# An encoder block on one core: row weights on K, three Q/K chains interleaved, gate weights ahead of branches, the last gate group by token halves

## The chip, the core and the metric

The kernel runs on one core of one Trainium2 chip. The engines are TensorE (PE in the profile; its weight loads are PEld), VectorE (DVE), ScalarE (ACT), GpSimd (POOL) and SyncE (SP), which here issues every DMA. The metric is the device time of one execution in microseconds (us), lower is better.

## The reference

One layer of an encoder on 1024 tokens (a grid of 16 rows by 64 columns), width 1024, all in float32:

```
u = rmsnorm(x) * g1
q, k, v, cb, cc, ch, ga, gb = split(u @ w_in)     # 512 each, ga and gb 1024 each
q = rmsnorm(q per head) * gq ; k = rmsnorm(k per head) * gk       # 8 heads of 64
p = softmax(q k^T / 8 + bias) in a window of 8 rows x 16 columns, clamped to the grid
y_a = (p v) @ w_a                                  # attention branch
y_b = (cb * conv3(cc * ch)) @ w_b                  # convolution branch
x = x + (sigmoid(ga) * y_a + sigmoid(gb) * y_b) @ w_o
x = x + relu(rmsnorm(x) * g2 @ w1)^2 @ w2          # feed-forward width 4096
```

## The kernel before, in words

**Split products.** Every large product is taken in float16 with float32 sums. Each operand is scaled by a power of two and split into a high half (ScalarE writes the rounded copy) and a low half (VectorE subtracts the high half from the scaled value, `scalar_tensor_tensor`). Three matmuls per tile pair (`PASSES`) add high-high, high-low and low-high. A *unit* is the matmuls of one output tile in one PSUM bank; `unit()` issues them, counts them in `units`, and then runs pending work of the other engines. Text and profile call such groups units: 24 matmuls in the projections, 12 in the gates and branches.

**Order of the work.** The whole order is written out: Python generators yield between instructions and are advanced by hand. `fg` holds work that follows a unit (`step()` advances every generator of it by one), `bg` holds the preparation of weights (`tick()` advances the first one, and, where `side` is set, the next ones while the first yields `WAIT`). `unit(mms, post, steps, ticks)` settles the `post` of the unit before, then takes `steps` steps and `ticks` ticks in turn. `apart(mark, n)` yields `WAIT` until `units` has reached `mark + n`; `flush()` runs `bg` empty with such waits set aside (`forced`). Each engine takes its instructions in the order of issue.

**Weights.** `plan()` gives the order of the weight pieces. `load_upto` loads them in that order into a ring of five raw buffers (`raw`, L205, on SP's queue); a piece is loaded when `done` counts enough split pieces (L205 can then wait for its buffer). `Chunk.prep` (L236 to L285) makes the scale of a chunk: for Q, K, the convolution and gate 0 by sums of squares over rows (L236 squares on ScalarE, L239 the sum), the sum over partitions by a matmul with ones (L176), `pow2_half` (L399 to L406) and the row scale (L248); then it splits the pieces (L285 high, L273 low). Between the sum of rows and the matmul with ones stands `yield from apart(units[0])`, three units. For the branches, w_o and V the scale comes from largest values (L296 to L306).

**Stages.** (1) Norm of x, transposes (L432 by DMA for blocks 3 to 7), V; from x also four *token forms* (sums and differences of quarters, `sforms`, L469 the scaled copies, L476 on GpSimd, L478 high, L480 low half, L482 stored to `GS` in DRAM), which the gates use. (2) Q: 8 units, K: 8 units. Each has a chain `qk_vec` behind it: copy (L570), squares (L571), sums per head (L574), reciprocal root (L385 to L394), a scale `sgq` for Q (L578), product (L581), the gains gq times gk for Q (L584), high half (L588, `q16`; for Q written twice), low half (L590); `finish_qk` then transposes the block by DMA (L601). (3) Two convolution units, then attention in 64 steps with the convolution's matmuls among them (180 to 357 us). (4) Gate stage: eight groups n of 128 columns; each has gate units, then four branch units. Group 0 is taken directly, groups 1 to 7 by seven products instead of eight (Strassen and Winograd): `prep_s` scales and adds raw weights (L973, L941), sums them, and splits them (L960 high, L954 low); `seven()` issues units 1, 6, 5, 4, 2, 7, 3, each with an activation form f and a weight form w. `turn_s` brings the stored forms back transposed (L909); form f = 2 lies where half of u was, and comes after group 0's gates. `post7` and `post3` close the group, `sigmoid` (L1026) runs over all four quarters. (5) Group 7 takes its branches first, into `y`; `last()` multiplies gate and y and `m_split` splits the result (L994, L996) into `M`. (6) Projection w_o in two column halves of eight token blocks; the first two units issue 21 of 24 matmuls each before the three that need group 7. Norm and the feed-forward part (from about 690 us) follow.

Of the kernel before, what the change touches and what calls it, by code (L numbers as in the profile page):

```python
# [10 lines left out]
F32 = mybir.dt.float32  # L11
F16 = mybir.dt.float16
# [3 lines left out]
OP = mybir.AluOpType  # L16
# [5 lines left out]
HD = 64  # L22
# [6 lines left out]
def plan():  # L29


    def block(w, groups, per=2, tiles=8, first=0):
        return [(w, first + k, per, groups) for k in range(0, tiles, per)]

    p = [(("V", j), block("w_in", [(1024 + 256 * j, 256)], 4)) for j in range(2)]
    p += [(("Q", 0), block("w_in", [(0, 512)])), (("K", 0), block("w_in", [(512, 512)]))]
    p += [(("C", j), block("w_in", [(c + 128 * j, 128) for c in (2048, 2560, 1536)])) for j in range(4)]
    branch = lambda j: [((k, j), block(w, [(256 * j, 256)], 4, 4)) for k, w in (("A", "w_a"), ("B", "w_b"))]
    for n in range(8):
        p.append((("S" if n else "G", n), block("w_in", [(3072 + 128 * n, 128), (4096 + 128 * n, 128)], 4)))  # L40
        if n in (0, 1, 3, 5):
            p += branch((n + 1) // 2)
    p += [(("O", j), block("w_o", [(512 * j, 512)])) for j in range(2)]
    for q in range(16):
        p.append((("1", q), block("w_1", [(128 * q, 128), (2048 + 128 * q, 128)], 4)))
    for s in range(4):
        p.append((("2", s), [("w_2", 4 * s + k, 2, [(c, 512)]) for c in (0, 512) for k in (0, 2)]))
        p.append((("X", s), [("w_2", 16 + 4 * s + k, 2, [(c, 512)]) for c in (0, 512) for k in (0, 2)]))
    return p
# [3 lines left out]
def encoder_block(ctx: ExitStack, tc: tile.TileContext, x, weights, cols, gqk, g2, rel, masks, out):  # L53
# [161 lines left out]
    class Chunk:  # L215
# [9 lines left out]
        def prep(self):  # L225
# [5 lines left out]
            if self.kind in "QKCG":  # L231
                self.parts = wsp.tile([128, 2, tot], F16, name="w16_ws", tag="ws")
                for p, (k, w) in enumerate(self.widths):
                    while len(self.raw) <= p:
                        yield WAIT
                    A.activation(self.parts[:, 1, :k * w].bitcast(BF16), self.raw[p][:, :k * w], AF.Square,  # L236
                                 accum_out=sc[:, at(rm, p)])
                    yield
                V.tensor_reduce(sc[:, a], sc[:, at(rm, 0, n)], axis=AX, op=OP.add)  # L239
                c = ones_col()  # L240
                V.tensor_tensor(c, sc[:, a], sc[:, gm2], op=OP.mult)
                yield from apart(units[0])
                yield from all_sum(c, b, bank(self.bank) if self.bank else anybank(), 1e-36)
                yield from pow2_half(b, 14, s, self.inv, more=self.more)
            else:
                yield from self.largest(rm, a, b)
                yield from pow2(b, 14, s, self.inv, False, more=self.more)
# [211 lines left out]
    turned, formed = [0], [0]  # L459
    SFORM = (5, 8, 10, 12)  # L460

    def sforms():

        for n, start in enumerate(SFORM):
# [3 lines left out]
            for b in (n, n + 4):  # L468
                A.activation(xt[:, b], xt[:, b], AF.Copy, scale=sc[:, at(ys, b)])  # L469
                z += [xt[:, b, :512], xt[:, b, 512:]]  # L470
            yield
            f = wqk.tile([128, 4, 512], F32, name="sform", bufs=1)
            v = wqk.tile([128, 4, 2, 512], F16, name="s16", bufs=2)
            for o, a, b, op in ((2, z[0], z[2], OP.subtract), (0, z[2], z[3], OP.subtract),
                                (1, f[:, 0], z[0], OP.subtract), (3, z[1], f[:, 1], OP.add)):
                G.tensor_tensor(f[:, o], a, b, op=op)  # L476
            yield from apart(units[0], 1 + (start < 6))
            A.activation(v[:, :, 0], f, AF.Copy)  # L478
            yield
            V.tensor_tensor(v[:, :, 1], f, v[:, :, 0], op=OP.subtract)  # L480
            yield from apart(units[0], 1)
            SP.dma_start(GS[:, n], v)  # L482
            formed[0] = n + 1

# [82 lines left out]
    def qk_vec(ps, inv, kind, res):  # L567
        qs = wqk.tile([128, 512], F32, name="qs", bufs=2)
        sq = wqk.tile([128, 512], F32, name="sq", bufs=1)
# [5 lines left out]
        yield  # L575
        yield from rstd(ss, HD, y, 0 if kind == "q" else 12)
        if kind == "q":
            V.tensor_scalar(sc[:, y], sc[:, y], sc[:, sgq], None, op0=OP.mult)  # L578
            yield
        q3 = qs.rearrange("p (h d) -> p h d", h=8)  # L580
        V.tensor_tensor(q3, q3, sc[:, y][:, :, None].to_broadcast([128, 8, HD]), op=OP.mult)  # L581
        yield
        if kind == "q":
            V.tensor_tensor(q3, q3, gq[:, 0][:, None, :].to_broadcast([128, 8, HD]), op=OP.mult)  # L584
        r = 2 if kind == "q" else 1
        t = wqk.tile([128, 8, 2, r, HD], F16, name=kind + "16")
        q4 = q3[:, :, None, :].to_broadcast([128, 8, r, HD])
# [15 lines left out]
    for n, (kind, b) in enumerate(todo):  # L603
# [6 lines left out]
        def post(ps=ps, kind=kind, n=n, ch=ch):  # L610
            fg.append(qk_vec(ps, ch.inv, kind, q16[n]))
        unit(tok_mms(ps, actU, b, ch, 8, 512, 0), post, 6, 3)
        if n == 3:
# [368 lines left out]

    def seven(P, act, c0, c1, posts, steps, ticks):

        ps = {}
        for i, f, w in ((1, 0, 0), (6, 4, 5), (5, 2, 3), (4, 3, 6), (2, 1, 1), (7, 5, 4), (3, 6, 2)):
            ps[i] = anybank()[:, c0:c1]
            post = posts.get(i)
            unit(group(ps[i], [(P[:, w, sw, k * 128:k * 128 + 128], act(f, sa, k)[:, c0:c1])
                               for k in range(4) for sw, sa in PASSES]),  # L990
                 post and (lambda post=post: post(ps)), steps, ticks)
# [13 lines left out]
    def gate_units(n, tail=None):  # L1005
# [12 lines left out]
        def post7(ps):  # L1018
            V.tensor_tensor(z[2], ps[7], z[1], op=OP.add)
            V.tensor_tensor(z[1], z[3], z[1], op=OP.subtract)  # L1020
            V.tensor_tensor(z[3], z[3], z[2], op=OP.subtract)
            V.tensor_tensor(z[2], ps[4], z[2], op=OP.add)

        def post3(ps):
            V.tensor_tensor(z[1], ps[3], z[1], op=OP.add)
            A.activation(sg, sg, AF.Sigmoid, scale=sc[:, cS[n].inv])  # L1026
            if tail:
                tail()
        seven(cS[n].P, actS, 0, 512, {
# [3 lines left out]
            2: lambda ps: V.tensor_tensor(z[0], ps[2], z[0], op=OP.add),  # L1033
            7: post7, 3: post3}, 2, 4 if n < 7 else 6)
        return sg
# [10 lines left out]
    for n in range(8):  # L1046
        built(cG if n == 0 else cS[n])
        if n < 7:
            bg.insert(len(bg) if n == 0 else 0, prep_s(n + 1))
        if n in (2, 4):  # L1050
            push(cA[n // 2 + 1], cB[n // 2 + 1])
        m = w3p.tile([128, 2, 512], F32, name="m", bufs=1)
        mf = m.rearrange("p a t -> p (a t)")
        if n < 7:
# [9 lines left out]
            branch_units(n, post)  # L1064
            if n == 0:
                push(cA[1], cB[1])
            late.append(lambda n=n, mf=mf: fg.append(m_done(n, mf)))
        else:
# [20 lines left out]

            def last():  # L1090
                for half in range(2):
                    o = slice(2 * half, 2 * half + 2)
                    V.tensor_tensor(sg7[0][:, o], sg7[0][:, o], y[:, o], op=OP.mult)
                    V.tensor_tensor(m[:, half], sg7[0][:, 2 * half], sg7[0][:, 2 * half + 1], op=OP.add)
                fg.append(m_split(7, mf, s7))
            sg7 = []
            sg7.append(gate_units(7))
            X1 = base.tile([128, 8, D], F32, name="x1", tag="Q")
            for b in range(8):
                SP.dma_start(X1[:, b], x[b * 128:(b + 1) * 128, :])  # L1100
            settle()
            last()
    drain()
# [128 lines left out]
    two = []  # L1232
    for b in range(2):
        proj(b, 0, None, two)
    unit(two[0][0][:21])
    unit(two[1][0][:21])
    for mm, fin in two:
        unit(mm[21:], fin, 6, 3)
    for b in range(2, 8):
        proj(b, 0)  # L1240
# [311 lines left out]
```

## Time and profile before

| what | us |
|---|---|
| median of 3 runs (1317.94 to 1324.43) | 1320.93 |
| the profiled execution, its time | 1319.66 |
| its span, first to last instruction | 1317.9 |
| TensorE busy | 1226.5 (93%) |
| VectorE busy | 970.5 (74%) |
| ScalarE busy | 717.3 (54%) |
| GpSimd busy | 442.1 (34%) |

Busy times by stretch of the span (us; the clock is the granted TensorE clock as a share of full speed):

| stretch | stage | TensorE | VectorE | ScalarE | clock |
|---|---|---|---|---|---|
| 68 to 118 | Q | 45.3 of 50 | 34.2 | 30.0 | 0.93 |
| 118 to 180 | K, two convolution units | 55.2 of 62 | 49.6 | 37.6 | 0.94 |
| 180 to 357 | attention | 159.0 of 177 | 133.6 | 120.0 | 0.99 |
| 357 to 388 | gate group 0 | 31.0 of 31 | 11.3 | 18.1 | 1.00 |
| 388 to 432 | group 1, start of 2 | 37.8 of 44 | 30.3 | 21.9 | 0.92 |
| 432 to 598 | groups 2 to 7 | 166.0 of 166 | 120.1 | 74.9 | 1.00 |
| 598 to 690 | w_o | 85.5 of 92 | 64.6 | 36.6 | 0.98 |
| 690 to 1318 | norm, feed-forward | 595.3 of 628 | 485.6 | 333.1 | 0.97 |

A busy TensorE is not a TensorE at full speed: after an idle time matmuls show a lower clock and take longer. In a line of the profile, `L273` is a line of the kernel, `w_ws<-raw` says that it writes tile w_ws from raw, and a bracket gives the idle time of the engine before it and what ended it.

### The profile page before, as it was taken

The numbers are of one execution on the slowest core, as the hardware profiler recorded it, in microseconds if no ns is written. First come the engines' busy times: TensorE is split into PE (matmuls) and PEld (weight loads), VectorE is DVE, ScalarE is ACT, GpSimd is POOL, SyncE is SP. The second block draws the span as 40 slices with busy tenths as digits, with TensorE's granted clock in tenths as the row PEclk, the third lists the DMA queues.
The fourth block names the chain that finished last, engine by engine and source line by source line (L and its number), as shares of the span: only waits on it lengthen the run. The fifth ranks groups of instructions, "written<-read, shape, count | busy, mean of one in ns | idle before, by whom it ended". The sixth has DMA issues, their size and how long they took to land.

```text
span 1317.9 us, 16922 instructions
## 1 busy us (share of the span) xinstructions
PE 1226.5 (93%) x6294; PEld 581.5 (44%) x6294; DVE 970.5 (74%) x1747; ACT 717.3 (54%) x1057; POOL 442.1 (34%) x269
## 2 busy tenths in 40 slices
PE   5987998988998999998997899999999799999998
PEld 3533444444443444443445644444444344444443
DVE  6567867878646877665779777777846578889797
ACT  5765666667455555522445556655564664546530
POOL 2430001211121221100202587777837307080562
PEclk8989999999999999999997999999999899999999
DMA  6645545555653212105346554445461862626212
GB/s 242 143 148 116 117 105 125 119 96 128 125 111 96 78 39 64 44 21 207 96 93 135 148 175 132 163 147 176 176 239 67 270 253 69 251 96 240 68 60 96
DMA packets 170946, 173.86 MB, mean 132 GB/s; under 512 B 131440, under 2 KB 131952, under 8 KB 166768
## 3 DMA queue, kind: packets, MB, share of 16 engines
q1 hardware_dynamic: 170864, 172.79, 44.2%
q8 instruction: 49, 0.80, 0.2%
q14 instruction: 33, 0.27, 0.1%
HBM read 103.03 MB, written 37.75 MB: 107 GB/s over the span
## 4 chain that ended last, share of the span: by engine, by line
PE 48%; DVE 21%; ACT 12%; issue 9%; DMA 6%; POOL 2%; SPq 1%; ACTq 0%; DVEq 0%; POOLq 0%
PE ps_s L184 16%; PE ps_d L184 15%; PE ps_o L184 11%; PE ps_d L847 4%; DMA PT<-P 3%; DVE w L954 3%; ACT as L1257 2%; ACT w L960 2%; DVE as L1284 2%; DVE w_ws L273 1%; POOL sform L476 1%; DMA raw<-in_weights 1%; DVE v L1157 1%; DVE as L1289 1%; PE ps_s L771 1%
## 5 line engine op out<-in xcount | busy, mean ns | idle before, releaser
L184 PEld LDWEIGHTS <-w 128*128 128x128 f16 x1512 | 149.8, 100 | 163.9 <-issue 18.3
L184 PEld LDWEIGHTS <-ops 128*128 128x128 f16 x1356 | 133.2, 99 | 174.3 <-issue 19.0
L1124 POOL TENSOR_TENSOR as<-as 128x512 f32<-128x512 f32 x64 | 109.1, 1705 | 85.1 <-ACT as L1259 81.4
L847 PE MATMUL ps_d<-uT,w_ws 128*128 128x512 f16 x528 | 127.2, 382 | 0.9 <-ACT w_ws L285 0.8
L184 PE MATMUL ps_s<-ops 128*128 128x512 f16 (+1 forms) x528 | 119.7, 377 | 3.7 <-DVE x L1483 2.0
L184 PE MATMUL ps_d<-ops 128*128 128x512 f16 x492 | 113.4, 380 | 0.0
L941 POOL TENSOR_TENSOR tsum<-raw 128x512 f32<-128x512 f32 x32 | 57.9, 1827 | 146.4 <-DVE mL L996 68.1
L184 PEld LDWEIGHTS <-uT 128*128 128x128 f16 x648 | 65.9, 102 | 82.0 <-issue 22.9
L184 PEld LDWEIGHTS <-w_s 128*128 128x128 f16 x588 | 57.3, 99 | 78.6 <-issue 4.6
L184 PE MATMUL ps_d<-u2T,w 128*128 128x512 f16 (+1 forms) x396 | 85.7, 367 | 4.8 <-DVE as L1288 4.8
L1257 ACT ACTIVATE as<-as 128x2048 f32<-128x2048 f32 x16 | 30.6, 1910 | 108.7 <-DVE as L1292 108.7
L1373 ACT ACTIVATE ops<-hf,sc 128x2048 f16<-128x2048 f32 x26 | 51.9, 1997 | 67.2 <-PE ps_d L184 25.1
L184 PE MATMUL ps_o<-ops 128*128 128x512 f16 x336 | 79.9, 388 | 8.9 <-DVE ops L1382 4.7
L954 DVE SCALAR_TENSOR_TENSOR w<-raw,sc,w 128x512 f16<-128x512 f32 (+1 forms) x32 | 43.3, 1359 | 56.3 <-ACT w L960 56.2
L1375 DVE SCALAR_TENSOR_TENSOR ops<-hf,sc,ops 128x2048 f16<-128x2048 f32 x26 | 70.2, 2699 | 12.8 <-ACT ops L1373 12.8
L847 PEld LDWEIGHTS <-w_ws 128*128 128x128 f16 x528 | 51.1, 98 | 56.4 <-issue 3.3
L1388 POOL TENSOR_TENSOR raw<-raw 128x1024 f32<-128x1024 f32 x8 | 24.8, 3095 | 142.8 <-DVE ops L1382 142.8
L941 POOL TENSOR_TENSOR gsum<-raw 128x512 f32<-128x512 f32 x14 | 18.6, 1329 | 138.9 <-ACT raw L973 138.9
L184 PE MATMUL ps_d<-w_ws,uT 128*128 128x512 f16 x192 | 49.3, 410 | 11.5 <-DVE w_ws L273 8.1
L954 DVE SCALAR_TENSOR_TENSOR w<-tsum,sc,w 128x1024 f16<-128x1024 f32 x32 | 59.5, 1896 | 0.0
L184 PE MATMUL ps_s<-u2T,w 128*128 128x512 f16 (+1 forms) x252 | 50.0, 350 | 2.8 <-DVE form L1150 2.8
L941 POOL TENSOR_TENSOR tsum<-tsum,raw 128x512 f32<-128x512 f32 x32 | 46.1, 1439 | 18.1 <-ACT tsum L936 16.8
(290 smaller groups left out, 2591.9 us busy)
## 6 DMA issues: line engine op xcount, KB each, us to landing
raw<-in_weights SPq DMA_DIRECT2D x92, 512.0 KB, 3.8
hs<-as SPq DMA_DIRECT2D x16, 1792.0 KB, 6.8
hf<-hs SPq DMA_DIRECT2D x26, 1024.0 KB, 9.5
w2x<-in_weights SPq DMA_DIRECT2D x16, 512.0 KB, 7.5
raw<-in_weights SPq DMA_DIRECT2D x16, 384.0 KB, 3.3
xt<-in_x SPq DMA_DIRECT2D x8, 512.0 KB, 9.9
gs<-s SPq DMA_DIRECT2D x4, 1024.0 KB, 4.3
x<-in_x SPq DMA_DIRECT2D x8, 512.0 KB, 9.4
```

What stands on the lines that cost most here:

```text
L184: T.matmul(ps, l, r, start=a, stop=b)
L273: V.scalar_tensor_tensor(lo, self.raw[p][:, o:o + m], sc[:, c:c + 1], hi, op0=OP.mult, op1=OP.subtract)
L847: T.matmul(ps, l, r, start=a, stop=b)
L941: G.tensor_tensor(t[:, o], a, b, op=OP.add)
L954: V.scalar_tensor_tensor(P[:, a:b, 1], w, sc[:, s], P[:, a:b, 0], op0=OP.mult, op1=OP.subtract)
L960: A.activation(P[:, a:b, 0], w, AF.Copy, scale=sc[:, s])
L1124: sub.tensor_tensor(z[o], z[a], z[b], op=op)
L1257: A.activation(f[:, 0:4], f[:, 0:4], AF.Relu)
L1284: V.tensor_tensor(z[1], z[3], z[5], op=OP.subtract)
L1373: A.activation(P[:, 1, 0], hf, AF.Copy, scale=sc[:, Rs])
L1375: V.scalar_tensor_tensor(P[:, 1, 1], hf, sc[:, Rs], P[:, 1, 0], op0=OP.mult, op1=OP.subtract)
L1388: G.tensor_tensor(w11[i2], w11[i2], w12[i2], op=OP.add)
```

## The change

- **Q and K.** The factor sgq and the gains gq times gk go on K instead of Q, with the constants of both roots exchanged. A unit is followed by four steps instead of six, so that a chain runs over three units; `qs` has three buffers; the results of Q and K share one ring (tag `q16`) of two.
- **Sums of rows.** For Q the matmul with ones stands two units behind the sum of rows, for the other chunks three as before.
- **Token forms.** The first starts a unit later; GpSimd's work is issued right behind the scaled copies; the high half follows two units behind the start; the store is its own generator, so that the next form may start before it.
- **Loads.** In `plan()` the branch pieces j come behind gate group 2j (before: behind groups 0, 1, 3, 5). `prep_s` is appended to `bg`, not put ahead of it, and branch chunks are pushed in groups 1, 3 and 5 (before: 0, 2, 4).
- **Gate units.** The order is 1, 6, 2, 4, 5, 7, 3.
- **Group 7.** Once unit 7 is in, the second token half is closed: sigmoid, product with y, sum, split. Unit 3 closes the first half. The projection starts with token blocks 4 and 5, then 6, 7, 0, 1, 2, 3.

```diff
@@ plan
-        if n in (0, 1, 3, 5):
-            p += branch((n + 1) // 2)
+        if n % 2 == 0:
+            p += branch(n // 2)
@@ Chunk.prep
-                yield from apart(units[0])
+                yield from apart(units[0], 2 if self.kind == "Q" else 3)
@@ sforms
-    SFORM = (5, 8, 10, 12)
+    SFORM = (6, 8, 10, 12)
...
-            yield
             f = wqk.tile([128, 4, 512], F32, name="sform", bufs=1)
...
-            yield from apart(units[0], 1 + (start < 6))
+            yield from apart(start, 2)
             A.activation(v[:, :, 0], f, AF.Copy)
             yield
             V.tensor_tensor(v[:, :, 1], f, v[:, :, 0], op=OP.subtract)
-            yield from apart(units[0], 1)
-            SP.dma_start(GS[:, n], v)
-            formed[0] = n + 1
+            fg.append(sform_store(n, v))
+
+    def sform_store(n, v):
+        yield from apart(units[0], 1)
+        SP.dma_start(GS[:, n], v)
+        formed[0] = n + 1
@@ qk_vec
-        qs = wqk.tile([128, 512], F32, name="qs", bufs=2)
+        qs = wqk.tile([128, 512], F32, name="qs", bufs=3)
...
-        yield from rstd(ss, HD, y, 0 if kind == "q" else 12)
-        if kind == "q":
+        yield from rstd(ss, HD, y, 12 if kind == "q" else 0)
+        if kind == "k":
             V.tensor_scalar(sc[:, y], sc[:, y], sc[:, sgq], None, op0=OP.mult)
...
-        if kind == "q":
+        if kind == "k":
             V.tensor_tensor(q3, q3, gq[:, 0][:, None, :].to_broadcast([128, 8, HD]), op=OP.mult)
         r = 2 if kind == "q" else 1
-        t = wqk.tile([128, 8, 2, r, HD], F16, name=kind + "16")
+        t = wqk.tile([128, 8, 2, r, HD], F16, name=kind + "16", tag="q16")
...
-        unit(tok_mms(ps, actU, b, ch, 8, 512, 0), post, 6, 3)
+        unit(tok_mms(ps, actU, b, ch, 8, 512, 0), post, 4, 3)
@@ seven
-        for i, f, w in ((1, 0, 0), (6, 4, 5), (5, 2, 3), (4, 3, 6), (2, 1, 1), (7, 5, 4), (3, 6, 2)):
+        for i in order:
+            f, w = SEVEN[i]
@@ gate_units
             V.tensor_tensor(z[2], ps[4], z[2], op=OP.add)
+            if tail:
+                A.activation(sg[:, 2:], sg[:, 2:], AF.Sigmoid, scale=sc[:, cS[n].inv])
+                tail(sg, 1)
 
         def post3(ps):
             V.tensor_tensor(z[1], ps[3], z[1], op=OP.add)
-            A.activation(sg, sg, AF.Sigmoid, scale=sc[:, cS[n].inv])
+            c = 2 if tail else 4
+            A.activation(sg[:, :c], sg[:, :c], AF.Sigmoid, scale=sc[:, cS[n].inv])
             if tail:
-                tail()
+                tail(sg, 0)
...
-            7: post7, 3: post3}, 2, 4 if n < 7 else 6)
+            7: post7, 3: post3}, 2, 4 if n < 7 else 6, (1, 6, 2, 4, 5, 7, 3))
@@ the loop over groups
-            bg.insert(len(bg) if n == 0 else 0, prep_s(n + 1))
-        if n in (2, 4):
+            bg.append(prep_s(n + 1))
+        if n in (1, 3, 5):
             push(cA[n // 2 + 1], cB[n // 2 + 1])
...
-            if n == 0:
-                push(cA[1], cB[1])
...
-            def last():
-                for half in range(2):
-                    o = slice(2 * half, 2 * half + 2)
-                    V.tensor_tensor(sg7[0][:, o], sg7[0][:, o], y[:, o], op=OP.mult)
-                    V.tensor_tensor(m[:, half], sg7[0][:, 2 * half], sg7[0][:, 2 * half + 1], op=OP.add)
-                fg.append(m_split(7, mf, s7))
-            sg7 = []
-            sg7.append(gate_units(7))
+            def last(sg, half):
+                o = slice(2 * half, 2 * half + 2)
+                V.tensor_tensor(sg[:, o], sg[:, o], y[:, o], op=OP.mult)
+                V.tensor_tensor(m[:, half], sg[:, 2 * half], sg[:, 2 * half + 1], op=OP.add)
+                t = slice(512 * half, 512 * half + 512)
+                A.activation(M[0][:, 7, t], m[:, half], AF.Copy, scale=sc[:, s7])
+                V.scalar_tensor_tensor(M[1][:, 7, t], m[:, half], sc[:, s7], M[0][:, 7, t],
+                                       op0=OP.mult, op1=OP.subtract)
+
+            gate_units(7, last)
...
-            last()
@@ projection w_o, first column half
-    for b in range(2):
+    for b in (4, 5):
         proj(b, 0, None, two)
...
-    for b in range(2, 8):
+    for b in (6, 7, 0, 1, 2, 3):
         proj(b, 0)
```

3 lines of the change are left out of this document (2 added, 1 removed).

## The prediction

> **What bounds the kernel now.** The page's first part gives TensorE 93% of the span, so a change that leaves the matmuls alone can win back only TensorE's idle time and the slow matmuls after it. The list of waits says what TensorE waited for (split weights, a transposing DMA, the merged activations); its timeline says where. I count in units, one output tile each: 24 matmuls take 5.18 us undisturbed (start to start), 12 take 2.59 us. First the query/key stage; the columns are start and length in us, engine, line, operation, and in brackets the idle time before it with its releaser:
>
> ```profile
> 63.12 5.35 PE L184 MATMUL ps_s<-w_v,uT 128*128 128x512 f16 x24
> ...
> 81.36 5.34 PE L184 MATMUL ps_o<-w_ws,uT 128*128 128x512 f16 x24
> ...
> 112.46 5.34 PE L184 MATMUL ps_o<-w_ws,uT 128*128 128x512 f16 x24
> ...
> 133.36 5.34 PE L184 MATMUL ps_o<-w_ws,uT 128*128 128x512 f16 x24
> ```
>
> The last V unit is over at 68.3; the second Q unit starts at 81.36, so the first took 13.1 us: 7.9 lost. The last Q unit ends at 117.6 and the second K unit starts at 133.36: 15.7 us for the first, 10.5 lost. VectorE in this stage shows why:
>
> ```profile
> 60.32 0.14 DVE L403 TENSOR_SCALAR sc<-sc 128x1 int32<-128x1 int32 x1
> 66.08 2.29 DVE L480 TENSOR_TENSOR s<-sform,s 128x2048 f16<-128x2048 f32 x1 [5.61 <-ACT s L478]
> 68.28 0.15 DVE L405 TENSOR_SCALAR sc<-sc 128x1 int32<-128x1 int32 x1
> ...
> 73.27 7.60 DVE L273 SCALAR_TENSOR_TENSOR w_ws<-raw,sc,w_ws 128x512 f16<-128x512 f32 x6 [0.68 <-ACT w_ws L285]
> ...
> 102.45 0.68 DVE L581 TENSOR_TENSOR qs<-qs,sc 128x512 f32<-128x512 f32 x1
> ...
> 108.35 0.68 DVE L581 TENSOR_TENSOR qs<-qs,sc 128x512 f32<-128x512 f32 x1
> ```
>
> Q's scale (L403, L405) is cut in two by the low half of a token form (L480), which waits for ScalarE, which waits for GpSimd; so the split of Q's weights (L273) ends at 80.9. After that one Q chain takes 5.9 us (102.45 to 108.35), more than a unit's 5.18: two chains hand each other between VectorE and ScalarE with both idle in between. VectorE falls behind, and K's weights, queued behind the chains, are split only by 132.4. Then the gate stage:
>
> ```profile
> 397.37 3.85 PE L184 MATMUL ps_o<-uT,w_s 128*128 128x512 f16 x11 [0.85 <-DMA uT<-gs]
> ...
> 424.06 0.60 PE L184 MATMUL ps_s<-uT,w_s 128*128 128x512 f16 x2 [1.60 <-ACT w_s L960]
> ```
>
> Group 1 waits in its third unit for a form, group 2 at its start for its weights. Five units from 388.16 end at 406.65: 18.5 us against 13.0, 5.5 lost. Two units from 422.30 end at 432.43: 10.1 against 5.2, 4.95 lost. Group 2's raw weights stand in SP's queue behind the transposes of that form:
>
> ```profile
> 396.03 51.69 SPq L205 DMA_DIRECT2D raw<-in_weights  x9
> ```
>
> Last, the hand-over to the projection w_o, ScalarE and then VectorE:
>
> ```profile
> 596.96 5.01 ACT L285 ACTIVATE w_ws<-raw,sc 128x512 f16<-128x512 f32 x8 [8.10 <-DVE sc L248]
> 605.70 2.00 ACT L1026 ACTIVATE sg<-sg,sc 128x2048 f32<-128x2048 f32 x1 [3.73 <-DVE sg L1025]
> ```
> ```profile
> 599.68 5.38 DVE L273 SCALAR_TENSOR_TENSOR w_ws<-raw,sc,w_ws 128x512 f16<-128x512 f32 x8
> 604.98 0.68 DVE L1025 TENSOR_TENSOR sg<-ps_s,sg 128x512 f32<-128x512 f32 x1
> ```
>
> The weights are split first, the last gate is finished after them, and its low half is ready at 614.0. From the end of the gates at 598.44 the fourth projection unit starts at 621.52, where 614.0 was possible: 7.5 lost. All these losses together are 36.4 us; nothing more is to be had.
>
> **The change, part by part.**
>
> *Start of Q.* Q's sum of rows is done two units on instead of three: its matmul (57.84) moves to about 52.6. The forms start a unit later and issue their GpSimd work at once, so form 1's high half (L478) now stands in ScalarE's order behind Q's scale instead of ahead of it. Form 0: GpSimd about 49 to 54, its high half to 55.9, the copies of form 1 (2.1 us, L469) to 58.0, its low half (2.29) to 58.2, Q's scale right behind. The normalization of block 7 (L415, L417) now stands behind form 1's copies and is done at about 60.6 instead of 58.8; with 4.3 us for its transposing DMA the last V unit starts at 65.2 instead of 63.12 and ends at 70.4. That delay is covered by the splits. Q's first piece is split by about 66, form 1's low half runs to 68.3, and pieces 1 to 3 (six instructions) follow beside form 2's GpSimd work, at the 1.27 us each that the row at 73.27 shows under GpSimd (0.70 without): to 75.3. The last quarter of the first Q unit ends then at about 76.1 instead of 81.36: **-5.3**. Bounds: -6.8 (splits at 0.70 when ScalarE is ready), -1.7 (if form 1 still cuts in once, 3.6 later). The page "SBUF — State Buffer" of the Trainium skill (terms, shared port pair) says that VectorE and GpSimd hold a common port pair in turn and the loser is blocked for the whole instruction. By that rule six splits (4.05) and a form (5.0) would add to 9.05 from 68.3, Q's unit would end 1.5 later, this part would be -3.8 and the whole 1297; the trace (7.60 for the six while GpSimd took 6.1 for its form) is a little kinder, and I keep the row.
>
> *Q and K chains.* Q loses L578 and L584 (0.15 and 0.6 of VectorE's time), K gains them: nothing over both. Four steps a unit instead of six leave three chains in flight. In one unit's order VectorE then has L390, the low half (L590) of the oldest, L102, the sum (L574) of the newest, L394, L385, L581, L388, while ScalarE has the oldest's copy (1.06), the newest's two passes (0.67, 0.6) and a root. From one L581 to the next: copy 1.06, L590 1.2, sum 0.6, small ones 0.4, L581 0.6: 3.9 us, less than 5.18, so VectorE keeps up with TensorE. The forms still end in this stage, so chains 0 and 1 run late (to about 95); from the fifth unit on there is no lag. K's scale and splits stand in the seventh and eighth units' steps, as before, but these now run when TensorE gets there: with chain steps between, pieces 0 and 1 are split by 111 and the last by 116. TensorE ends Q at 112.5 and needs the last piece at 116.4. I give K's start 0.3 of stall: **-10.2**. Bounds: -10.5 and -4 (the splits alone, 5.4 us, wholly behind the end of Q, with the slow clock). The third buffer of qs serves the third chain; K's results share Q's ring of two, priced below.
>
> *Into attention.* K's chains are 0.75 longer and the last three are less advanced when K's units end; two convolution units (10.4) cover them. Block 15 is needed late. I take **+0.8**, between 0 and +3 (attention waited 8.9 us in all on VectorE's L785, so it has little slack there). The rest of attention I leave as it is: 18.0 us idle in 180 to 357, from causes that the change doesn't touch.
>
> *Gate order and loads.* With units in the order 1, 6, 2, 4, 5, 7, 3 the late form is used fifth: at 388.16 + 4 x 2.59 = 398.5, and its transposes land by 397.4. **-5.5** (bounds -5.5 and -3, if it lands 1 us late with slow matmuls after it). Group 2's two pieces take the queue places of branch pieces A1 and B1: issued at 346.8 and 384.4, not from 396.03. Its ScalarE work (L973 at 400.09) can start at 388.7, and its split no longer waits for A1's and B1's (they stood before it at 416.9 to 423.3). Sum two to three units on, about 401; split by 408; needed at about 417. **-4.95**, bounds -4.95 and -2. A1 and B1 come from 396 on, and are needed first by group 2's branches, 18 us after its start; VectorE was idle 394.5 to 405.7, which takes the displaced work. From 432 to 598 TensorE has no gap and VectorE is 72% busy: nothing.
>
> *Last gate by halves.* Half 1's sigmoid, products and low half now stand ahead of the weight pieces 1 to 3 on ScalarE and of all pieces on VectorE. From L1022's end at 599.76: sigmoid 1.1, product 1.23, sum 0.69, copy 0.6, low half 0.69: 604.3, with the waits between. Only then come the splits (5.38): 609.7. TensorE, idle from 598.7, gets its first low half at 605.0; the stall is 6.3 us where it was 1.65 and 3.2. After the 3.20 us stall matmuls ran at about 0.43 for some 4 us; so I take nine slow ones here: 21 + 21 matmuls to 616.1, six more to 617.4, fourth unit at 622.6 instead of 621.5: **+1.1**. The last half is long done. Bounds: -0.8 (no slow clock) and +3 (half 1 delayed by GpSimd or a queue). The x blocks (L1100) queue on SP behind raw loads that wait for those splits, and come 4.3 later; the first use was at 627.3, with landing near 620: covered.
>
> Sum: -5.3 - 10.2 + 0.8 - 5.5 - 4.95 + 1.1 = -24.1. The profiled execution took 1319.66 us, 0.1% under the median, so **1296 us**. The feed-forward part shifts whole.
>
> **Rivals.** (A) One of the two big parts stays: K's splits still come late, or group 2's weights do. If all the gain of K's start but 2 goes, -24.1 + 8.2 gives 1304; if the gate stage gives nothing, -24.1 + 10.4 gives 1306. For it: both rest on an order of issue that I worked out, not saw. Against: the waits named are exactly those moved. (B) Slower: the common ring of two for Q's and K's results. A chain's copy must wait until the transposing DMA of the chain two before has read its buffer. That makes the period half of copy, low half and landing: (2.3 + 4.5)/2 = 3.4 us now, harmless. It costs from 5.18 on, that is when landing takes over 8 us. The parts away from the chains give -13.9 (gate -10.45, Q's start -5.3, halves +1.1, into attention +0.8); 16 chains outweigh them at 0.9 more each, a period of 6.1 and landings of 9.9, which is where the sign turns. At 12 us, a period of 7.2, 16 x 2.0 = 32 lost against 13.9: 1338. All eight landings were 4.3 to 5.1, but SP also carries forms and weights in order. (C) No change in sum: attention gives it back, with its DMA transposes and VectorE as the real bound; it would have to grow by 24 us, more than all its idle time now, for chains that end at most 3 us later in their order. About 1318.
>
> **How the numbers follow.** My forecast 0.58, (A) 0.25, (B) 0.08, (C) 0.05, and 0.04 for a loss that I don't see. Forecast and A end below 1313; 0.5% (6.6 us) is about what a measurement can tell from no change. Parts of A with bad bounds and C make "same" 0.08, B and the unseen 0.10, the rest 0.82 faster. The range is the forecast's with its bounds (all at their best -28.6, 1291, and 5 of attention's 18 idle us, which a shifted start can move either way) up to both forms of A with 4 of the same: 1286 to 1310.
>
> **What would show it.** Right: second Q unit at about 76, no stall over 1 us before the second K unit, L581 to L581 no longer 5.9 but the unit's 5.18, no wait for uT<-gs and none for w_s at group 2, L273 of w_o after the half's low part with a TensorE stall of about 6 us there. Wrong: ScalarE's L588 waiting for a DMA (B), waits on L273 before K, or new gaps in attention.

## The result, and the profile after

The changed kernel took 1299.81 us (median of 4, 1297.96 to 1304.36) beside 1321.18 for the kernel before on the same chip (median of 4): a ratio of 0.984, 95% interval 0.981 to 0.988. The forecast was 1296, the range 1286 to 1310. So the sign and the size are right; the parts are not all, and they are told apart here by stages. The profiled execution of the changed kernel was its slowest, 1304.36 us (span 1302.6, clock 0.973). Line numbers of the changed kernel are 2 to 8 higher: the copy of a finished chain is L590 (before L588), its low half L592, the chain's product L583.

All stages are read from TensorE's timeline: the first matmul of each stage, in us from the span's start.

| from | to | before | after | difference | predicted |
|---|---|---|---|---|---|
| start | second Q unit | 81.36 | 77.82 | -3.5 | -5.3 |
| second Q unit | second K unit | 52.00 | 41.46 | -10.5 | -10.2 |
| second K unit | attention | 46.64 | 46.65 | 0.0 | 0 |
| attention | gate group 0 | 177.03 | 180.85 | +3.8 | +0.8 |
| group 1 | first w_o matmul | 210.28 | 199.79 | -10.5 | -10.45 |
| first w_o matmul | fourth projection unit | 23.08 | 23.67 | +0.6 | +1.1 |
| fourth projection unit | second column half | 25.96 | 29.82 | +3.9 | 0 |
| second column half | end | 670.42 | 671.41 | +1.0 | 0 |

(Gate group 0, 31.13 us, is the same in both. The code of the last row is the same in all kernels of this document; it took 667.1 to 672.4 us in their profiles, and the +1.0 lies within that.) The sum is -15.3, for one pair of profiles with the changed kernel at its slowest; the medians differ by 21.4.

The query/key stage, in TensorE's timeline of the changed kernel (columns as before: start, length, engine, line, operation, and in brackets the idle time ahead with its releaser):

```profile
65.58 6.97 PE L184 MATMUL ps_s<-w_v,uT 128*128 128x512 f16 x24 [2.37 <-DMA uT<-u]
72.39 5.60 PE L184 MATMUL ps_d<-w_ws,uT 128*128 128x512 f16 x24
77.82 5.34 PE L184 MATMUL ps_o<-w_ws,uT 128*128 128x512 f16 x24
...
108.92 5.34 PE L184 MATMUL ps_o<-w_ws,uT 128*128 128x512 f16 x24
114.11 5.34 PE L184 MATMUL ps_d<-w_ws,uT 128*128 128x512 f16 x24
119.28 5.34 PE L184 MATMUL ps_o<-w_ws,uT 128*128 128x512 f16 x24
```

From 72.39 on every unit, the last of Q and the first of K (114.11) among them, starts 5.2 to 5.4 us after the one before. The wait of V's last unit for its transpose is new (2.37). VectorE there:

```profile
61.75 0.14 DVE L403 TENSOR_SCALAR sc<-sc 128x1 int32<-128x1 int32 x1
61.92 0.15 DVE L405 TENSOR_SCALAR sc<-sc 128x1 int32<-128x1 int32 x1
...
67.02 2.29 DVE L479 TENSOR_TENSOR s<-sform,s 128x2048 f16<-128x2048 f32 x1 [0.74 <-ACT s L477]
69.23 1.41 DVE L273 SCALAR_TENSOR_TENSOR w_ws<-raw,sc,w_ws 128x512 f16<-128x512 f32 x2
70.94 6.40 DVE L273 SCALAR_TENSOR_TENSOR w_ws<-raw,sc,w_ws 128x512 f16<-128x512 f32 x4 [0.30 <-ACT w_ws L285]
```

Q's scale (L403, L405) is no longer cut in two. Two splits take 0.70 us each, the next four 1.6 each. The gate stage, as a row of busy times (stretch, length, busy TensorE, its weight loads, VectorE, ScalarE, GpSimd, granted clock, share and rate of the DMA):

```profile
377.91:577.70 199.79, 199.79 (x939) 90.61 (x937) 152.36 (x299) 96.98 (x154) 31.31 (x24) 1.00 0.20 60
577.70:631.19 53.49, 45.09 (x195) 19.56 (x194) 31.79 (x51) 15.76 (x23) 5.76 (x4) 0.90 0.44 158
```

From group 1 to w_o TensorE has no idle time at all; in the second row, w_o's first half, it loses 8.4 us and the clock is 0.90 on average. That stage, first on TensorE, then VectorE, then SP's queue:

```profile
584.45 0.58 PE L184 MATMUL ps_o<-w_ws,mH 128*128 128x512 f16 x1 [6.37 <-DVE w_ws L273]
...
613.92 0.16 PE L176 MATMUL ps_o<-ones 128*128 128x1 bf16 x1 [2.03 <-DVE ones L306]
```
```profile
582.98 0.75 DVE L1103 SCALAR_TENSOR_TENSOR mL<-m,sc,mH 128x512 f16<-128x512 f32 x1 [0.79 <-ACT mH L1102]
583.65 5.38 DVE L273 SCALAR_TENSOR_TENSOR w_ws<-raw,sc,w_ws 128x512 f16<-128x512 f32 x8
...
606.50 1.22 DVE L375 TENSOR_REDUCE sc<-g2b 128x1 f32<-128x1024 f32 x1 [12.16 <-DMA g2b<-in_g]
607.64 1.21 DVE L296 TENSOR_REDUCE sc<-raw 128x2 f32<-128x1024 f32 x1
```
```profile
585.12 4.27 SPq L205 DMA_DIRECT2D raw<-in_weights  x4
589.44 5.86 SPq L1109 DMA_DIRECT2D x<-in_x  x8
596.31 0.33 SPq L1121 DMA_DIRECT2D g2b<-in_g  x1
```

The splits now follow the finished half, and TensorE waits 6.37 us for them in one piece, as worked out (6.3). The second wait was not foreseen: the largest values of w_o's next weights (L296) stand in VectorE's order behind the reduction of g2 (L375), which waits 12.16 us for a load that SP issues only behind the weights and the blocks of x, 18.6 us after the end of the gates, and that lands 10.1 us after its issue. In the kernel before it was issued 15.7 us after the end of the gates (598.44):

```profile
614.11 0.33 SPq L1113 DMA_DIRECT2D g2b<-in_g  x1
```

### The profile page after: what moved, and what is told of

The parts are those of the page before. It is cut to its first block, busy times and chain, and to the rows that moved or that the text cites. A ratio compares the mean times of both kernels' runs of the same rounds, so it can differ in the third digit from the quotient of the medians.

```text
span 1302.6 us, 16912 instructions
## 1 busy us (share of the span) xinstructions
PE 1221.2 (94%) x6294; PEld 581.8 (45%) x6294; DVE 969.5 (74%) x1748; ACT 717.0 (55%) x1059; POOL 443.3 (34%) x269
## 4 chain that ended last, share of the span: by engine, by line
PE 53%; DVE 19%; ACT 10%; issue 9%; DMA 7%; POOL 2%; SPq 0%; DVEq 0%; ACTq 0%; POOLq 0%
PE ps_d L184 17%; PE ps_s L184 16%; PE ps_o L184 14%; PE ps_d L849 4%; DVE w L956 3%; DMA PT<-P 3%; ACT w L962 2%; ACT as L1265 2%; DVE as L1292 2%; DVE v L1165 1%; DMA u2x<-v 1%; DMA raw<-in_weights 1%; POOL sform L475 1%; DVE ops L1390 1%; DVE as L1297 1%
## 5 line engine op out<-in xcount | busy, mean ns | idle before, releaser
L184 PEld LDWEIGHTS <-uT 128*128 128x128 f16 x648 | 65.2, 101 | 68.0 <-issue 3.6
L943 POOL TENSOR_TENSOR gsum<-raw 128x512 f32<-128x512 f32 x14 | 18.6, 1335 | 133.5 <-ACT raw L975 118.8
L184 PE MATMUL ps_s<-u2x,w 128*128 128x512 f16 (+1 forms) x228 | 49.7, 370 | 3.4 <-DMA u2x<-v 3.4
```

The source lines that it names most:

```text
L184: T.matmul(ps, l, r, start=a, stop=b)
L943: G.tensor_tensor(t[:, o], a, b, op=OP.add)
```

## The experiments

### Where the w_o stage lost its time

The theory: two separate waits, one for splits queued behind the finished half, one for g2. Each was taken away alone; a third run took the whole last part back. First, g2's scale, appended later:

```diff
     push(cO[1])
-    fg.append(g2_scale())
...
     for b in (6, 7, 0, 1, 2, 3):
+        if b == 1:
+            fg.append(g2_scale())
         proj(b, 0)
```

> The changed kernel with one edit: the scaling of g2 (L375 and what follows it) is appended to the foreground work only ahead of block 1's projection, not ahead of all eight. Theory (the first half of w_o lost 4.4 us because VectorE's largest values for w_o's second half, L296, stood behind L375, which waited for the load of g2 to 606.5): the matmul with ones at 613.92 no longer waits (2.03 us) and its two neighbours run at full speed, so the time falls by 3.9 us, to about 1296. Rival (the raw weights themselves came late): the wait stays and the time stays at 1300.

It took 1298.29 us (ratio to the kernel before 0.983, 0.981 to 0.985), by the medians 1.5 us under the changed kernel, where 3.9 were expected. The two intervals overlap, so the time does not show the gain; the stage does. The wait for L306 is gone and the stage from the first w_o matmul to the second column half fell from 53.49 to 50.00 us. Of the 3.5, 2.2 lie ahead of the sixth unit (the wait), 1.7 behind it (slow matmuls), and the first four units took 0.4 more. The slow matmuls don't follow in every execution: in the run with six steps (under "Attention"), whose w_o code is the changed kernel's, the wait for L306 was 1.42 us, the matmuls behind it ran at full speed, and the stage took 51.65 us.

Second, the first finished half closed behind the splits, in `post3`:

```diff
             V.tensor_tensor(z[2], ps[4], z[2], op=OP.add)
-            if tail:
-                A.activation(sg[:, 2:], sg[:, 2:], AF.Sigmoid, scale=sc[:, cS[n].inv])
-                tail(sg, 1)
 
         def post3(ps):
+            if tail:
+                A.activation(sg[:, 2:], sg[:, 2:], AF.Sigmoid, scale=sc[:, cS[n].inv])
+                tail(sg, 1)
             V.tensor_tensor(z[1], ps[3], z[1], op=OP.add)
```

> The changed kernel with one edit: the second token half of group 7 is closed right ahead of the first one, behind the splits of w_o's weights, not ahead of them. Theory: the stall of 6.4 us ahead of the projection shrinks to about 1.7 and the fourth projection unit starts 6 us earlier; but g2 cannot land much earlier, so the wait on L306 grows from 2 to some 5 us and only about 3 us of the 6 arrive, 1297. Rival (the halves' order does not matter, the projection waits for group 7's low half as in the kernel before): a stall of 3 us at the last three matmuls and no gain, 1300.

1296.43 us (0.982, 0.980 to 0.983). The fourth projection unit starts 17.45 us after the first w_o matmul instead of 23.67; the wait for L306 is then met earlier and longer (3.78 us; 14.32 us for the next two units, where 10.39 are needed), and 48.98 us are left of 53.49.

Third, the last part as it was before, all others of the change kept:

```diff
-                tail(sg, 1)
...
-    for b in (4, 5):
+    for b in range(2):
...
-    for b in (6, 7, 0, 1, 2, 3):
+    for b in range(2, 8):
```

> The changed kernel with its last part taken back: group 7 is closed as in the kernel before, and the projection starts with blocks 0 and 1. The unit order and all the rest stay. Theory (this part costs 0.6 us at the start of the projection and 3.9 through the load of g2): faster than the whole change by 4.4 us, about 1295.5. Rival (the part helps, as the three matmuls that wait for group 7 no longer do): slower by 1 to 4 us, 1301 to 1304.

1298.40 us (0.983, 0.981 to 0.985), by the medians 1.4 us under the changed kernel, where 4.4 were expected; again the intervals overlap. The stage took 49.35 us. So in this stage the last part of the change, as made, cost 4.1 us in the changed kernel's profile and 2.3 in that of the run with six steps, and the other parts carry the whole gain. Both repairs together:

> The changed kernel with both repairs of the w_o stage: the scale of g2 ahead of token block 1's projection, and the first finished half closed behind the weight splits. Each alone took 3.5 and 4.5 us off the 53.49 us from the first w_o matmul to the second column half, but each left the other's wait. Theory: the two waits are separate; together the stage is 17.45 + 10.39 + 15.57 = 43.4 us, so the time is 10 us under the changed kernel's, 1290 (30 under the kernel before, ratio 0.977). Rival: the transfers of x and g2 collide with the split's loads whatever the order; then the stage stays near 47 and the time near 1294.

1293.01 us (median of 5; the kernel before 1318.54 there; 0.979, 0.977 to 0.981). Its row for the stage:

```profile
574.19:617.59 43.40, 41.74 (x195) 18.81 (x194) 32.12 (x51) 15.40 (x23) 5.60 (x4) 1.00 0.53 194
```

43.40 us, as expected, and not the rival's 47: the two waits are separate and both gone, the clock is 1.00. The kernel before took 49.04 here. In this stage the last part of the change is thus a gain of 5.6 us once its order is right, and as it was made a loss of 4.4 (2.6 in the run with six steps). The time alone would not have decided it: the expected ratio, 0.977, is the lower end of the interval, and the rival's 1294 us, 0.980, lies within it.

### Gate order and loads

Three runs on the kernel before: the order of the units alone, the order of the loads alone, and both.

```diff
-            7: post7, 3: post3}, 2, 4 if n < 7 else 6)
+            7: post7, 3: post3}, 2, 4 if n < 7 else 6, (1, 6, 2, 4, 5, 7, 3))
```

> The kernel before with the order 1, 6, 2, 4, 5, 7, 3 of the gate units alone. The gap in group 1 (5.5 us, wait uT<-gs) goes. Theory: the weights of group 2 come by their own chain, loaded from 396.03 on whatever TensorE does, so group 2 starts 5.5 us earlier and waits 5.5 us longer for w_s (about 10 instead of 4.95); time unchanged, 1320 us, and the two gate parts are no sum of two but one gain that needs both. Rival: the two are independent as the prediction counted them, the gap at group 2 stays near 5, and the time is 5.5 lower, 1315.

```diff
-        if n in (0, 1, 3, 5):
-            p += branch((n + 1) // 2)
+        if n % 2 == 0:
+            p += branch(n // 2)
...
-            bg.insert(len(bg) if n == 0 else 0, prep_s(n + 1))
-        if n in (2, 4):
+            bg.append(prep_s(n + 1))
+        if n in (1, 3, 5):
```

> The kernel before with the new order of loads alone, the gate units as before. The order of units alone gained nothing (210.76 us from group 1 to w_o against 210.28), both together 10.5. Theory: group 1 keeps its gap of 5.5 us and group 2 finds its weights ready, so 205.3 us and a time 5 us under the kernel before. Rival: the pieces A1 and B1, now late, become the next wait, and nothing is gained without the order either (210).

> The kernel before with the unit order and the loads. Both gaps go: from the first gate unit of group 1 to the first w_o matmul 199.8 us instead of 210.3, as in the changed kernel; 1320.7 - 10.45 = 1310. If attention's lateness in the changed kernel came from the loads (pieces A1 and B1 no longer in it), attention is over 1 us longer here too; theory: it comes from the Q/K chains, and attention stays at 177.0 within 0.5.

| kernel | group 1 to first w_o matmul | ratio to before (interval) |
|---|---|---|
| before | 210.28 us | 1 |
| order alone | 210.76 | 1.003 (1.001 to 1.005) |
| loads alone | 204.90 | 0.996 (0.994 to 0.998) |
| both | 199.78 | 0.993 (0.991 to 0.996) |

TensorE's timeline with the order alone, and then with the loads alone:

```profile
407.16 0.16 PE L176 MATMUL ps_d<-ones 128*128 128x1 bf16 x1 [5.09 <-DVE ones L918]
...
431.51 2.33 PE L184 MATMUL ps_o<-qD,w_s 128*128 128x512 f16 x10 [2.21 <-DVE w_s L954]
```
```profile
395.71 0.39 PE L184 MATMUL ps_o<-uT,w_s 128*128 128x512 f16 x1 [2.16 <-DMA uT<-gs]
397.01 4.24 PE L184 MATMUL ps_o<-uT,w_s 128*128 128x512 f16 x11 [0.91 <-DMA uT<-gs]
```

The order alone takes the wait for the form (uT<-gs) away, and TensorE loses as much before group 2's weights: 5.09 us at the sum over partitions (L176), which stands in its instruction stream ahead of group 1's last two units, 2.5 us in the slow unit behind it, and 2.21 us for low halves. In time the order alone was even slower, 1321.79 us beside 1317.92, where no change was expected; 0.5 of these 3.9 us is seen in the stage, and the rest is not explained. The loads alone take 5.4 us off the stage, and the order is worth 5.1 more only on top of them.

### Q and K: chains or forms

The prediction said that two interleaved chains with a period of 5.9 us made VectorE late for K's weights. The rival: the token forms did. The chain part alone on the kernel before (its lines of `qk_vec` and the four steps), and then the sums and forms alone (its lines of `Chunk.prep`, `SFORM` and `sforms`):

```diff
-        qs = wqk.tile([128, 512], F32, name="qs", bufs=2)
+        qs = wqk.tile([128, 512], F32, name="qs", bufs=3)
...
-        if kind == "q":
+        if kind == "k":
...
-        unit(tok_mms(ps, actU, b, ch, 8, 512, 0), post, 6, 3)
+        unit(tok_mms(ps, actU, b, ch, 8, 512, 0), post, 4, 3)
```

> The kernel before with the Q/K part alone: weights on K, four steps, three buffers qs, common ring. Theory: the period of two interleaved chains made VectorE late for K's weights; so the first Q unit keeps its 7.9 us of loss, the distance from second Q to second K unit falls from 52.0 to about 41.5, and attention is 3 to 4 us longer (its last K block ends about 2.3 us later against attention's start, as in the changed kernel). In all 1320.7 - 10.5 + 3.5 = 1314, a little more if forms and chains now meet. Rival: the token forms, not the chains, hold VectorE; then the distance stays above 47 and the time above 1317. For attention: if the later K blocks are not from the chains, it stays near 177 and the time is 1310.

```diff
-                yield from apart(units[0])
+                yield from apart(units[0], 2 if self.kind == "Q" else 3)
...
-    SFORM = (5, 8, 10, 12)
+    SFORM = (6, 8, 10, 12)
```

> The kernel before with Q's sum two units on and the new timing of the token forms, chains as before. Theory: second Q unit at 76 to 78 instead of 81.4; the chains keep their period of 5.9 us, and VectorE is late for K's weights by its own order, so the distance from second Q to second K unit stays at 52 or grows by what Q won (up to 55); time between 1316 and 1320. Rival: the forms' end sets the lateness; they end some 4 us earlier, K's weights come that much earlier, and the distance falls to 48 or less: 1311 to 1313.

The chains alone: 1309.15 us beside 1317.92 (0.993, 0.991 to 0.996); from the second Q unit to the second K unit 41.46 us, exactly the changed kernel's, and the first Q unit as slow as before (11.85). The time fell by 8.8 us, where 6.7 were expected with an attention 3 to 4 us longer; attention took 178.62 us, 1.6 longer than before. The sums alone: 1317.31 (0.999, 0.997 to 1.001); the second Q unit at 77.00, and 50.95 us to the second K unit. VectorE's low half of the last token form (L480, L479) and the first products in the two kernels (the chains alone, then the sums alone; start, length, line):

```profile
92.81 2.29 DVE L480 TENSOR_TENSOR s<-sform,s 128x2048 f16<-128x2048 f32 x1 [3.29 <-ACT s L478]
...
95.89 0.69 DVE L581 TENSOR_TENSOR qs<-qs,sc 128x512 f32<-128x512 f32 x1
...
99.74 0.69 DVE L581 TENSOR_TENSOR qs<-qs,sc 128x512 f32<-128x512 f32 x1
```
```profile
88.47 2.29 DVE L479 TENSOR_TENSOR s<-sform,s 128x2048 f16<-128x2048 f32 x1 [0.99 <-ACT s L477]
...
91.41 0.68 DVE L583 TENSOR_TENSOR qs<-qs,sc 128x512 f32<-128x512 f32 x1
...
97.25 0.68 DVE L583 TENSOR_TENSOR qs<-qs,sc 128x512 f32<-128x512 f32 x1
```

3.9 us with three chains, which catches up on a backlog; 5.9 with two. The chains alone settle the question: the last form ends there 14.6 us after the second Q unit, as in the kernel before (95.97 against 81.36), and yet all of the lateness is gone, so the rival falls. The sums alone settle nothing: the last form ends 5.2 us earlier there, but the second Q unit starts 4.4 us earlier too, so against it the forms moved by 0.85 us and the distance shrank by 1.05, which the rival would have given as well. The forms still have a part: in both kernels the first product follows the low half of the last form by less than 1 us, so the forms make the backlog, and three chains clear it. Whether the factors on K, the four steps or the third buffer do it was not taken apart. What the sums win at Q's start is not seen in the time of that kernel: in its profile 4.4 us at Q and 1.1 more at K are followed by 0.9 more in attention and 1.8 more in the gate stage, which wasn't traced further, and the interval allows a gain of 3.7.

### Attention

Of the last K block, ScalarE's copy (L590), then VectorE's low half (L592) and the first score (L787), and GpSimd's first instruction (L676), in the changed kernel, whose attention starts at 165.93:

```profile
162.19 0.63 ACT L590 ACTIVATE k<-qs 128x512 f16<-128x512 f32 x1 [1.86 <-DMA kD<-k]
165.57 0.63 ACT L590 ACTIVATE k<-qs 128x512 f16<-128x512 f32 x1 [2.75 <-DVE qs L586]
```
```profile
166.24 0.69 DVE L592 TENSOR_TENSOR k<-qs,k 128x512 f16<-128x512 f32 x1 [0.70 <-ACT k L590]
...
170.20 0.48 DVE L787 CUSTOM_DVE_ANT_0 sz<-ps_s,bias,sc 128x256 f32<-128x256 f32 x1 [3.02 <-PE ps_s L773]
```
```profile
170.30 0.10 POOL L676 MEMSET z<- 128x1 f32 x1 [57.65 <-DMA kD<-k]
```

The first score starts 4.3 us after attention's first matmul; before it was 2.1. It does not wait for its data: TensorE's matmul for it, of the first K blocks, ran at 165.93. VectorE, ScalarE (L678, at 170.13) and GpSimd, whose memset reads nothing of K, all start just after the last transposing DMA of K lands (170.02), and so they do in the kernel before (landing at 181.76, first score at 182.11). Their tiles lie in the pool that is opened when the pool of the chains is closed (`pqk.close()`), so the reuse of that memory is the likely reason; no run kept the two pools apart. The distance stays: of the 64 exponentials (L807 before), the first came 9.56 us after attention's start before and 11.76 now, the 61st 160.99 and 163.47. First remedy: six steps for the last four K units.

```diff
-        unit(tok_mms(ps, actU, b, ch, 8, 512, 0), post, 4, 3)
+        unit(tok_mms(ps, actU, b, ch, 8, 512, 0), post, 6 if n > 11 else 4, 3)
```

> The changed kernel with one edit: the last four K units are followed by six steps, not four, so that fewer chain steps are left when K's units end. Theory (attention takes 180.9 us instead of 177.0 because the last K block is transposed 2.3 us later against its start, and a wait on convolution weights follows from it): attention falls to 177 to 178.5, the time by 2 to 4 us, about 1297. Rival (attention is longer for another reason, such as the loads): attention stays near 180.9 and the time at 1300.

A miss: 1301.71 us (0.986, 0.984 to 0.988). The last K block came 3.2 us later still, the first score at 7.4, the first and the 61st exponential 3.1 us later each (14.91 and 166.59), attention 181.65 us. It shows the dependence on that block, with the wrong sign of the remedy: the copy waited 3.9 us for the transposing DMA instead of 1.9, and the splits of the convolution's weights, in the same steps, moved later too. What follows the 61st exponential took 15.1 to 17.4 us in the thirteen profiles, so the length of a single attention says less than its first score. Second remedy, on the kernel with both repairs: more buffers for K's results (`qk_vec` is given the number n of the block).

```diff
-        t = wqk.tile([128, 8, 2, r, HD], F16, name=kind + "16", tag="q16")
+        t = wqk.tile([128, 8, 2, r, HD], F16, name=kind + "16", tag="s16" if kind == "k" and n % 2 else "q16")
```

> The kernel of the run above with every second K block's result in the buffers that the token forms have left: four results of K in flight instead of two. Theory: ScalarE's copy of the second last K block waits 1.9 us for the transposing DMA of the block two before, which stands behind 4.6 us of weight loads in SP's queue; without that wait the last K block ends 1.9 us earlier (at -0.9 instead of +1.0 us against attention's first matmul), the first score comes at +2.4 instead of +4.3, and attention is 1.9 us shorter (about 178.4); time 1.9 us under the run above. Rival: SP's queue itself is the limit (the transposes stand behind the loads anyway), the first score stays at +4.3 and nothing is gained.

1290.83 us (0.978, 0.975 to 0.980), the fastest of all; from its neighbour with both repairs (0.979, 0.977 to 0.981) the intervals don't part it. The copy's wait for the DMA is gone, but a wait of 1.17 us for VectorE (L586) stands in its place, and the first score comes at 3.75 instead of 4.30: 0.55 us of the 1.9 expected. The 61st exponential comes 0.54 us earlier too, while attention as a whole took 179.61 us in this profile and 178.61 in its neighbour's. So the ring of two delays the scores by about half a microsecond here. It is not new: K's results had two buffers before as well, and the same copy waited 2.84 us for the DMA there. The chain itself, less advanced when K's units end, is left for most of the lateness; that was not taken away in a run and stays argued.

How much of attention's +3.8 is the change? Kernels that leave Q and K as before took 177.03, 177.15, 178.56 and 178.72 us for attention (before, loads, order, both gate parts), and 177.90 with the sums alone. The 178.72 misses what was expected of both gate parts, 177.0 within 0.5, but the order of the gate units alone, which changes nothing up to there, took as long. With the order alone the same copy of K waited 4.49 us for the DMA instead of 2.84:

```profile
174.92 0.63 ACT L588 ACTIVATE k<-qs 128x512 f16<-128x512 f32 x1 [4.49 <-DMA kD<-k]
```

With the whole Q/K part it took 178.61 to 180.85 (the chains alone, the changed kernel and four of its variants, without the two remedies). The means are 177.9 and 179.8. So some 1.9 us belong to the change, about the lateness of the first score (2.2), and the rest is the scatter of single executions.

## Why the prediction was right or wrong

**K's start (predicted -10.2): right.** -10.5 in the pair of profiles, and from the chains alone. The stall of 0.3 was not there. The period was no steady 5.18: the eight Q products of the changed kernel stand 3.8 to 7.9 us apart, 5.0 on average.

**Gate order and loads (-5.5 and -4.95): the sum right, the split wrong.** -10.5 was measured. But the first step, that the order alone gives 5.5, is refuted: it gives nothing while group 2's weights come by their own clock. The two terms are the loads, 5.4, and the order on top of them, 5.1.

**Start of Q (-5.3): right in kind, too large.** -3.5 in the pair; the mean over the five kernels with the old sums is 80.95, over the eight with the new 76.98: -4.0. The steps that were off: the last six splits started 0.9 us late, since form 1's low half ended at 69.2 and not at 68.3, and they took 8.1 us from there, where I put 7.0; six at the 1.27 us that I named make 7.6 already. By "SBUF — State Buffer" of the Trainium skill (terms, shared port pair), as the prediction estimated, the six and a form would have added to 9.05; the measured 8.1 lies between that rule and my row, and by the rule the term would have been -3.8. The wait of V's last unit, at 65.58 as worked out (65.2), was covered by the splits as claimed: the unit then took 6.97 us here and 5.35 in the kernel with both repairs, and from its start to the second Q unit it was 12.24 us in both.

**Into attention (+0.8, bounds 0 to +3): right in kind, mis-sized.** About +1.9, as just told. The step that failed is "two convolution units cover them": the last low half ended 1.3 us ahead of attention before and 1.0 behind its start now. And "Block 15 is needed late" holds for its scores alone: VectorE, ScalarE and GpSimd started attention only when that block had been transposed.

**Last gate by halves (+1.1): right to half a microsecond.** The stall was 6.37 us (6.3 predicted), the fourth unit at +0.6. So a loss here was foreseen; that it could be turned around by leaving the early close to `post3` was not.

**"The x blocks come 4.3 later: covered": wrong, and the largest miss of the pair.** +3.9 us (+1.6 in the run with six steps). I followed the x blocks to their own use and not to the load that stands behind them on SP, g2, nor to what VectorE has queued behind the reduction of g2. In relation to the end of the gates its issue moved from 15.7 to 18.6 us and TensorE met a wait of 2.03 us, with slow matmuls behind it.

**The rivals.** (A), one big part failing, did not happen. (B) was seen as a wait of 1.9 us, once, at the end of K (0.55 us in the first score). Its sign, a copy that waits for a DMA, stood there in the kernel before too (2.84 us), so it could not tell the two apart. The landings of Q's and K's transposes were 3.1 to 6.1 us, under the 8 at which a period would cost. (C) is out: attention gave back 2 us, not 24. With the measured sizes, -4.0 - 10.5 + 1.9 - 10.5 + 4.45, the sum is -18.7, and -20.5 with the +2.6 that w_o cost in the run with six steps; the comparison gives 1 - 0.984 of 1320, 21 with an interval of about 16 to 25. The three mis-sized terms (Q's start by 1.3, attention by 1.1, w_o by 1.5 to 3.4) come to 3.9 to 5.8 us, and the forecast was 4 us too low.

## What to carry to other kernels

Where one wait is removed ahead of another in the same in-order stream, price the second wait again from the new time: the order of the gate units was worth 0 or 5.1 us, depending on the next weights. When a step is moved later, follow every DMA behind it in the issuing queue up to its user, and then what is queued behind that user on its engine; here a reduction of g2 that could as well run later held up weights that were needed at once. And finish half a result early only where it doesn't stand ahead of what the next stage starts with.

## What the hardware showed unexpectedly

The same stall cost different amounts in different executions. V's last unit waited 2.34 to 2.38 us in all eight kernels with the new sums; in four its matmuls then ran at full speed, in the other four slow. The changed kernel's line stands first in its query/key timeline above; this is the kernel with both repairs:

```profile
64.22 5.35 PE L184 MATMUL ps_s<-w_v,uT 128*128 128x512 f16 x24 [2.37 <-DMA uT<-u]
```

24 matmuls took 6.97 us there (granted clock 0.76 on average) and 5.35 here (1.00), after 2.37 us of waiting each time. "TensorE: Matmul & The Clock Gate" of the Trainium skill (Part 1, "What's actually happening") has the clock fall after an idle window of about 3.4 us, whose position is free; the free position agrees with the four and four, the length does not, since no wholly idle window of 3.4 us fits into 2.37. So a stall of this size is best priced with both ends, 0 and 1.6 us here, beyond its own length.

The 1.27 us per split that the prediction took from the row at 73.27 mixes two prices. Of the six splits in that row, four ran beside GpSimd's form and took 1.25, 1.76, 1.75 and 1.75 us, and two came behind it and took 0.74. In the changed kernel the last six were two of 0.74 us ahead of the form, and beside it 1.38 and three times 1.75. So the price of the overlap was the same in both kernels; a mean over a row hides it, and what has to be worked out is how many splits fall beside the form.
